# Output projection of two mixers: partial sums of three token tiles kept in PSUM banks, and two places for the first MLP weights' work

## The chip, the cores and the metric

One core of a Trainium2 chip. The metric is the device time of one execution in microseconds (us); lower is better. Engines: PE (TensorE, matmul), DVE (VectorE), ACT (ScalarE), POOL (GpSimd), SP (SyncE, which issues most DMAs). Time before: 1218.78 us, median of 3 runs (1217.87 to 1219.89).

## The reference

A two-layer decoder trunk for 512 tokens of width 1024, in float32.

```python
for layer in range(DEPTH):                      # DEPTH = 2
    hn = rmsnorm(h, mix_norm[layer])
    if layer % 2 == 0:
        h = h + moba_nsa_mixer(hn, ...)         # 8 MoBA and 8 NSA heads
    else:
        h = h + fox_mixer(hn, ...)              # 16 heads, forgetting attention
    h = h + sqrelu_mlp(rmsnorm(h, mlp_norm[layer]), mlp_w1[layer], mlp_w2[layer])
return rmsnorm(h, final_norm)
```

Both mixers end in `o @ w_out`: all heads' outputs, 512 x 1024, times a 1024 x 1024 matrix. `sqrelu_mlp` is `relu(h @ w1)**2 @ w2` with 4096 hidden columns.

## The kernel before

The stages follow each other: mixer 0 to about 315 us, its MLP to about 640, the forgetting attention ("fox") to about 885, the second MLP to the end. The residual stream stands in four tiles `x0` to `x3` of 128 tokens x 1024. A float32 product is made of three matmuls (`mm3`, L142 to L144): each operand is split into a rounded high part and a low part, and high x low, low x high and high x high are added in one PSUM bank. High parts of weights are copies on ACT (L100), low parts a subtraction on DVE or POOL (L107); `whl` holds both.

PSUM has eight banks here: four tags (`acc`, `s`, `pt`, `o`) of two buffers each. `acc` takes sums of projections, `s` logits (L544, L583), `pt` transposes (L566, L395) and also logits of fox, `o` the heads' outputs (L639, L662).

Output projection (`out_proj`): heads go in pairs, of which there are eight; a pair is 128 rows of `w_out`. For given pairs, token tile t and half n of the 1024 columns, three matmuls per pair add into one `acc` bank, and DVE adds the bank to `x` (L711, 128x512). An operation `o45:012` does this for pairs 4 and 5 and tiles 0 to 2. Mixer 0 ends with pairs 2 and 3, whose heads come last; fox ends with 6 and 7. A pair's output is split before: in mixer 0 by ACT (L680), DVE (L681) and POOL (L533, L689), in fox by ACT (L672) and DVE (L673).

Then comes the MLP: each tile x is squared and summed on ACT (L383), a scale `nr` comes of it (L386 to L388, DVE), x is multiplied by it and the norm's weights (L390, DVE, `xn`), transposed on PE through `pt` banks (L395), and copied to float16 high and low parts by ACT (L398) and DVE (L399).

The first MLP weights are prepared within the mixer before: `s0` to `s3` (mixer 0 only) load one of four 128-column blocks and square it on ACT (L441) for a scale; `x` loads them again, and `z0` to `z3` (`prepare_part`, `up_split`) make their high float16 part on ACT (L477) and the low part on DVE (L478). An instruction tied by `issue_after` stands in its engine's queue no earlier than the one named. `prepare_part` ties its two to `a_last` and `ev_last`; `ev_last` is the last addition to x so far.

The order of all this is written in two strings, whose words run from left to right: the scheduler sets each instruction by the order written, the ties and the readiness of its data, and each engine then works off its queue in order. Other words: `n`, `m` attention of a pair of NSA or MoBA heads, `k`, `q`, `v` projections, `c` compressed branch, `t` scales, `p` a pair of fox heads.

Of the kernel before, what the change touches and what calls it, by code (L numbers as in the profile page):

```python
# [12 lines left out]
ALU = mybir.AluOpType  # L13
# [31 lines left out]

MIX0_ORDER = "c0 k1 q1 s0 n0 v1 s1 v0 s2 k0 s3 n1 m1 c1 t m0 k2 n2 o45:0123 o0:0123 n3 k3 m2 m3 o17:0123 o6:012 o23:0 x0 z0 o23:1 z1 o6:3 z2 o23:2 z3 o23:3"

FOX_ORDER = "v0 f k0 k1 p0 k2 v1 p1 k3 p2 o01:0123 k4 v2 p3 k5 p4 k6 v3 p5 k7 p6 o23:0123 p7 o45:012 o67:0 x1 z0 o67:1 z1 o45:3 z2 o67:2 z3 o67:3"

# [5 lines left out]
class Trunk:  # L55
    def __init__(self, ctx, tc, I, out):
# [3 lines left out]
        self.phase = "D"  # L60
        self.wout = {}
        e = ctx.enter_context
        PS = bass.MemoryType.PSUM
# [23 lines left out]
    def split(self, srcs, shape, pool):  # L87
# [10 lines left out]
        def parts(squares=None):  # L98
            hl = (pool or self.whl).tile([P, 2, W_RAW], FR, tag="whl", name=self.nm("whl"))
            nc.scalar.activation(hl[:, 0, :n], raw[:, :n], AF.Copy)  # L100
            if squares is not None:
                c, scratch, out = squares
                scratch = (hl[:, 1] if scratch is None else scratch)[:, :n].rearrange("p (a b) -> p a b", a=a)
                nc.scalar.activation(scratch[:, :, :c], rv[:, :, :c], AF.Square, accum_out=out)
            eng = nc.gpsimd if self.phase[self.pieces % len(self.phase)] == "P" else nc.vector
            self.pieces += 1
            eng.tensor_tensor(hl[:, 1, :n], raw[:, :n], hl[:, 0, :n].bitcast(F32), op=ALU.subtract)  # L107
            hv = hl[:, :, :n].rearrange("p t (a b) -> p t a b", a=a)
            return [(hv[:, 0, i], hv[:, 1, i]) for i in range(a)]
# [378 lines left out]
    def prepare_mlp(self, layer):  # L488
# [5 lines left out]
        def part(f):  # L494
            self.first_up.extend(self.up_split(raws[f:f + 1], self.up_first[layer][:, :, f:f + 1], tiles[f:f + 1], [(self.a_last, self.ev_last)]))
        self.prepare_part = part
# [38 lines left out]
    def softmax(self, passes, band, gate):  # L535
# [4 lines left out]
        for qi in range(NT):  # L540
            w = P * (qi + 1)
            ps = self.psum("s")
            for i, (q, k) in enumerate(passes):
                nc.tensor.matmul(ps[:, :w], q[:, qi * P:(qi + 1) * P], k[:, :w],  # L544
                                 start=i == 0, stop=i == len(passes) - 1)
            seg = pt[:, SEG[qi]:SEG[qi] + w]
# [7 lines left out]
    def transpose_p(self, p):  # L554
# [4 lines left out]
        for off, js in BANKS:  # L559
            pt = self.psum("pt")  # L560
            w = 0
            for j, c in js:
                for qi in range(j, NT):
                    a = SEG[qi] + j * P
                    b = c + (qi - j) * P
                    nc.tensor.transpose(pt[:, b:b + P], p[:, a:a + P], self.ident)  # L566
                    w = max(w, b + P)
# [4 lines left out]
    def softmax_t(self, passes, band):  # L572
# [6 lines left out]
        for qi in (3, 2, 1, 0):  # L579
            w = P * (qi + 1)  # L580
            ps = self.psum("s" if qi % 2 else "pt")
            for i, (q, k) in enumerate(passes):
                nc.tensor.matmul(ps[:, :w], q[:, qi * P:(qi + 1) * P], k[:, :w],  # L583
                                 start=i == 0, stop=i == len(passes) - 1)
            seg = pt[:, SEG[qi]:SEG[qi] + w]
# [105 lines left out]

    def out_proj(self, w, arg, os, hs, late, pools={}):

        nc = self.nc
        pairs, tiles = ([int(a) for a in part] for part in arg.split(":"))
        phase = self.phase
        if tiles[0] == 0:
            for i in pairs:
                self.phase = "P" if i in late else "D"
                self.wout[i] = self.rows(w, P * i, 1, pools.get(i))[0]  # L700
                self.phase = phase
        for t in tiles:
            for n in range(2):
                ps = self.psum("acc")
                for k, i in enumerate(pairs):
                    o, wc = os[i], self.wout[i]
                    self.mm3(ps, (o[:, 0, t * P:(t + 1) * P], o[:, 1, t * P:(t + 1) * P]),
                             (wc[0][:, n * 512:(n + 1) * 512], wc[1][:, n * 512:(n + 1) * 512]),
                             k == 0, k == len(pairs) - 1)
                hv = hs[t][:, n * 512:(n + 1) * 512]  # L710
                self.ev_last = nc.vector.tensor_tensor(hv, ps, hv, op=ALU.add)  # L711

# [63 lines left out]
    def mixer0(self):  # L776
# [5 lines left out]
        with ExitStack() as cx:  # L782
# [210 lines left out]
            def step(op, arg):  # L993
# [21 lines left out]
                elif op == "m":  # L1015
                    o[int(arg)] = moba_pair(int(arg), *k[int(arg)])
                elif op == "o":
                    self.out_proj(wo, arg, o, hs, ())

# [148 lines left out]
    def mlp(self, layer, hs, final=None):  # L1168
# [6 lines left out]
        with ExitStack() as cx:  # L1175
# [161 lines left out]
            def down(s, act):  # L1337
                bs = combos(act)
                if s < 6:
                    late = 4 * [(self.up_done[3],)] if ahead < 3 else [(done,) for done in self.up_done]  # L1340
                    if s == 1 and ahead < 4:
                        self.up_squares(*loaded[3], up_sq[1], self.parts_last)
                        scale[3] = up_scale(3, "acc")
                    up_split(s + 2, self.added if s else self.first_low, late if s + 2 < 4 else None)
                bank = {}
# [77 lines left out]
    def fox(self, hs):  # L1423
# [5 lines left out]
        with ExitStack() as cx:  # L1429
# [124 lines left out]
            def step(op, arg):  # L1554
# [11 lines left out]
                elif op == "p":  # L1566
                    pair(int(arg), st[int(arg)])
                elif op == "o":
                    if int(arg.split(":")[0][-1]) not in o:
                        with self.tc.issue_after(self.mm_last.ins):  # L1570
                            behind()
                    self.out_proj(wo, arg, o, hs, (6, 7), {7: last})

# [43 lines left out]
```

## Time and profile before

| | |
|---|---|
| median of 3 runs | 1218.78 us |
| the profiled execution | 1221.25 us |
| its span | 1219.5 us |
| granted PE clock | 0.994 |
| additions to x (L711) | 72, median 689 ns |

A row of a timeline gives start (us from the span's start), duration in us, engine, line, operation, output and inputs with shapes, and in square brackets the idle time of the engine just before it with what ended it. In a table of windows each engine has its busy time and number of instructions; PEclk is the granted clock as a share of the full one.

### The profile page before, as it was taken

The numbers are of one execution on the slowest core, as the hardware profiler recorded it, in microseconds if no ns is written. First come the engines' busy times: TensorE is split into PE (matmuls) and PEld (weight loads), VectorE is DVE, ScalarE is ACT, GpSimd is POOL, SyncE is SP. The second block draws the span as 40 slices with busy tenths as digits, with TensorE's granted clock in tenths as the row PEclk, the third lists the DMA queues.
The fourth block names the chain that finished last, engine by engine and source line by source line (L and its number), as shares of the span: only waits on it lengthen the run. The fifth ranks groups of instructions, "written<-read, shape, count | busy, mean of one in ns | idle before, by whom it ended". The sixth has DMA issues, their size and how long they took to land.

```text
span 1219.5 us, 17282 instructions
## 1 busy us (share of the span) xinstructions
PE 1183.5 (97%) x6197; PEld 870.3 (71%) x6197; DVE 937.9 (77%) x1741; ACT 734.3 (60%) x1347; POOL 323.5 (27%) x387
## 2 busy tenths in 40 slices
PE   9999998998999999999999999999999999999997
PEld 7878987886755665665588888787675666656666
DVE  6867778897879778876977685777787697779865
ACT  6456756784386676767524874676357555656442
POOL 3434555461041111121001643434003102201104
PEclk9999999999999999999999999999999999999999
DMA  8972242124323474456105473636644233442101
GB/s 234 330 227 80 70 129 70 44 61 121 87 87 115 127 207 140 117 158 212 33 1 154 105 161 88 153 92 139 183 138 138 87 104 87 138 121 71 68 1 70
DMA packets 204531, 144.78 MB, mean 119 GB/s; under 512 B 48484, under 2 KB 179724, under 8 KB 204445
## 3 DMA queue, kind: packets, MB, share of 16 engines
q1 hardware_dynamic: 204284, 143.44, 41.7%
q8 instruction: 49, 0.80, 0.3%
q14 instruction: 38, 0.30, 0.1%
q10 hardware_dynamic: 160, 0.23, 0.1%
HBM read 130.76 MB, written 7.64 MB: 113 GB/s over the span
## 4 chain that ended last, share of the span: by engine, by line
PE 77%; DVE 11%; DMA 5%; ACT 4%; issue 2%; POOL 1%; ACTq 0%; DVEq 0%; POOLq 0%; SPq 0%
PE acc L142 14%; PE acc L143 14%; PE acc L144 14%; PE s L1361 12%; PE o L1361 6%; PE pt L1361 3%; PE o L639 2%; PE pt L566 2%; PE s L544 2%; DVE whl L107 1%; DMA w<-in_mlp_w 1%; DMA HT<-HL 1%; PE s L144 1%; PE s L143 1%; PE s L142 1%
## 5 line engine op out<-in xcount | busy, mean ns | idle before, releaser
L142 PE MATMUL acc<-x,w 128*128 128x512 f16 (+1 forms) x512 | 187.8, 368 | 0.4 <-ACT r L1250 0.3
L143 PE MATMUL acc<-x,w 128*128 128x512 f16 (+1 forms) x512 | 187.7, 367 | 0.3 <-DVE nr L387 0.3
L144 PE MATMUL acc<-x,w 128*128 128x512 f16 (+1 forms) x512 | 187.5, 367 | 0.0
L1361 PE MATMUL s<-whl,sp 128*128 128x512 f32 x672 | 177.9, 406 | 0.0
L1361 PEld LDWEIGHTS s<-whl,sp 128*128 128x128 f32 x672 | 126.3, 188 | 31.0 <-DVE x L1370 0.5
L1309 ACT ACTIVATE whl<-w 128x1024 fp32r<-128x1024 f32 x98 | 100.3, 1048 | 65.5 <-DVE w L1315 40.5
L1370 DVE SCALAR_TENSOR_TENSOR x<-s,nr,x 128x512 f32<-128x512 f32 x112 | 82.6, 745 | 67.7 <-PE s L1361 67.5
L1310 DVE TENSOR_TENSOR whl<-w,whl 128x1024 fp32r<-128x1024 f32 x98 | 121.5, 1257 | 9.8 <-ACT whl L1309 9.7
L100 ACT ACTIVATE whl<-raw 128x1024 fp32r<-128x1024 f32 (+1 forms) x75 | 77.6, 1043 | 45.6 <-PE acc L144 16.6
L142 PEld LDWEIGHTS <-w 128*128 128x128 f16 x576 | 57.3, 100 | 57.6 <-issue 10.3
L1276 POOL TENSOR_TENSOR t<-act 128x512 f32<-128x512 f32 x14 | 24.8, 1772 | 274.0 <-ACT act L1252 251.0
L142 PE MATMUL acc<-xhi,whl 128*128 128x512 f32 x240 | 94.8, 395 | 1.7 <-DVE QS L529 0.8
L144 PEld LDWEIGHTS <-w 128*128 128x128 f16 x576 | 56.5, 98 | 55.6 <-issue 4.5
L144 PE MATMUL acc<-xhi,whl 128*128 128x512 f32 x240 | 94.2, 393 | 0.5 <-DVE whl L107 0.4
L143 PE MATMUL acc<-xlo,whl 128*128 128x512 f32 x240 | 94.0, 391 | 0.0
L143 PEld LDWEIGHTS <-w 128*128 128x128 f16 x576 | 56.6, 98 | 51.6 <-issue 4.5
L1361 PE MATMUL o<-whl,sp 128*128 128x512 f32 x336 | 84.8, 396 | 2.0 <-DVE x L1370 1.4
L107 DVE TENSOR_TENSOR whl<-raw,whl 128x1024 fp32r<-128x1024 f32 (+2 forms) x58 | 72.7, 1259 | 14.0 <-ACT whl L100 10.1
L1315 DVE TENSOR_TENSOR w<-w,w 128x1024 f32<-128x1024 f32 x56 | 72.2, 1289 | 5.0 <-DMA w<-in_mlp_w 4.6
L1250 ACT ACTIVATE r<-acc,upsc 128x512 f32<-128x512 f32 x44 | 30.0, 681 | 76.1 <-PE acc L144 76.0
L1361 PEld LDWEIGHTS o<-whl,sp 128*128 128x128 f32 x336 | 62.9, 188 | 16.5 <-DVE x L1370 1.8
L549 ACT ACTIVATE P<-P,sst 128x384 f32<-128x384 f32 (+2 forms) x96 | 53.4, 557 | 22.4 <-DVE sst L548 21.8
(346 smaller groups left out, 2910.0 us busy)
## 6 DMA issues: line engine op xcount, KB each, us to landing
w<-in_mlp_w SPq DMA_DIRECT2D x140, 512.0 KB
raw<-in_odd_w_in SPq DMA_DIRECT2D x22, 512.0 KB
raw<-in_even_w_in SPq DMA_DIRECT2D x20, 512.0 KB
band<-bias_dram SPq DMA_DIRECT2D x24, 256.0 KB
bias_dram<-bias_rows SPq DMA_DIRECT2D x16, 320.0 KB
raw<-in_even_w_out SPq DMA_DIRECT2D x8, 512.0 KB
raw<-in_mlp_w SPq DMA_DIRECT2D x8, 512.0 KB
raw<-in_odd_w_out SPq DMA_DIRECT2D x8, 512.0 KB
```

What stands on the lines that cost most here:

```text
L100: nc.scalar.activation(hl[:, 0, :n], raw[:, :n], AF.Copy)
L107: eng.tensor_tensor(hl[:, 1, :n], raw[:, :n], hl[:, 0, :n].bitcast(F32), op=ALU.subtract)
L142: mm(ps, ahl[0], bhl[0], start=first, stop=False)
L143: mm(ps, ahl[0], bhl[1], start=False, stop=False)
L144: self.mm_last = mm(ps, ahl[1], bhl[0], start=False, stop=last)
L549: nc.scalar.activation(seg, seg, AF.Exp, bias=mn, scale=-1.0, accum_out=sm)
L1250: nc.scalar.activation(r, ps, AF.Relu, scale=undo[:, 1, f:f + 1])
L1309: nc.scalar.activation(t[:, 0], src, AF.Copy)
L1310: nc.vector.tensor_tensor(t[:, 1], src, t[:, 0].bitcast(F32), op=ALU.subtract)
L1315: nc.vector.tensor_tensor(out, a_, b_, op=op)
L1361: mm = lambda l, r, first, last: nc.tensor.matmul(ps, l, r, start=first, stop=last, skip_group_check=True)
L1370: self.added = nc.vector.scalar_tensor_tensor(hv, ps, by_token(t), hv, op0=ALU.mult, op1=ALU.add)
```

## The change

In both strings the operation `o` is taken apart at the ends:

- `w45` loads and splits the output weights of pairs 4 and 5 (`out_rows`); before, the first `o` of a pair did this.
- `a6:1:s` opens the sums of pair 6 and tile 1 in the two banks of tag `s` and leaves them open; the matmuls are tied behind the last matmul, logit or transpose that uses the tag.
- `b23:1` adds pairs 2 and 3 to tile 1's open banks, and then DVE adds them to x.
- `o623:3` is as before, with all pairs left over for tile 3 in one sum.

At each end three tiles hold `acc`, `s` and `pt`, six banks. Additions to x fall from 16 to 8 at each end. The number of matmuls is the same.

Besides: `s0` to `s3` stand later in mixer 0. For the second layer `prepare_part` ties to the last high copy on ACT (`high_last`) in place of `a_last`. In the first MLP one tie of a weight split is dropped. `h` names the place where fox's follow-up (`behind`) is issued.

```diff
-MIX0_ORDER = "c0 k1 q1 s0 n0 v1 s1 v0 s2 k0 s3 n1 m1 c1 t m0 k2 n2 o45:0123 o0:0123 n3 k3 m2 m3 o17:0123 o6:012 o23:0 x0 z0 o23:1 z1 o6:3 z2 o23:2 z3 o23:3"
-FOX_ORDER = "v0 f k0 k1 p0 k2 v1 p1 k3 p2 o01:0123 k4 v2 p3 k5 p4 k6 v3 p5 k7 p6 o23:0123 p7 o45:012 o67:0 x1 z0 o67:1 z1 o45:3 z2 o67:2 z3 o67:3"
+MIX0_ORDER = "c0 k1 q1 n0 v1 v0 s0 k0 s1 n1 s2 m1 s3 c1 t m0 k2 n2 w45 o45:0123 w0 o0:0123 n3 k3 m2 m3 w17 o17:0123 w6 a6:0:acc a6:1:s a6:2:pt w23 x0 z0 z1 b23:0 z2 b23:1 z3 b23:2 o623:3"
+FOX_ORDER = "v0 f k0 k1 p0 k2 v1 p1 k3 p2 w01 o01:0123 k4 v2 p3 k5 p4 k6 v3 p5 k7 p6 w23 o23:0123 p7 w45 a45:0:acc a45:1:s a45:2:pt w67 x1 z0 z1 h b67:0 z2 b67:1 z3 b67:2 o4567:3"
...
-            nc.scalar.activation(hl[:, 0, :n], raw[:, :n], AF.Copy)
+            self.high_last = nc.scalar.activation(hl[:, 0, :n], raw[:, :n], AF.Copy)
...
-            self.first_up.extend(self.up_split(raws[f:f + 1], self.up_first[layer][:, :, f:f + 1], tiles[f:f + 1], [(self.a_last, self.ev_last)]))
+            self.first_up.extend(self.up_split(raws[f:f + 1], self.up_first[layer][:, :, f:f + 1], tiles[f:f + 1], [((self.high_last if layer else self.a_last), self.ev_last)]))
...
+    def out_part(self, ps, n, t, pairs, os, first, last):
+        for k, i in enumerate(pairs):
+            o, wc = os[i], self.wout[i]
+            self.mm3(ps, (o[:, 0, t * P:(t + 1) * P], o[:, 1, t * P:(t + 1) * P]),
+                     (wc[0][:, n * 512:(n + 1) * 512], wc[1][:, n * 512:(n + 1) * 512]),
+                     first and k == 0, last and k == len(pairs) - 1)
+
+    def out_proj(self, op, arg, os, hs):
...
+            if op == "a":
+                behind = {"acc": self.mm_last, "s": self.logit_last, "pt": self.turn_last or self.logit_last}[tag[0]]
+                for n in range(2):
+                    self.part[t, n] = ps = self.psum(tag[0])
+                    with self.tc.issue_after(behind.ins):
+                        self.out_part(ps, n, t, pairs, os, True, False)
+            elif op == "b":
+                for i in pairs:
+                    for n in range(2):
+                        with self.tc.issue_after(self.mm_last.ins):
+                            self.out_part(self.part[t, n], n, t, [i], os, False, i == pairs[-1])
+                for n in range(2):
+                    self.out_add(self.part.pop((t, n)), n, t, hs)
...
+    def out_add(self, ps, n, t, hs):
+        hv = hs[t][:, n * 512:(n + 1) * 512]
+        self.ev_last = self.nc.vector.tensor_tensor(hv, ps, hv, op=ALU.add)
...
-                    up_split(s + 2, self.added if s else self.first_low, late if s + 2 < 4 else None)
+                    up_split(s + 2, self.added if s else self.first_low, late if s + 2 < 4 and not (s and ahead < 4) else None)
```

The lines of the changed kernel are one higher up to the output projection (L107 becomes L108, L478 becomes L479), and the addition to x is L734 in place of L711.

**DVE, end of mixer 0.** `PTl` is the low part of the last head pair's transposed attention weights, which PE needs for that pair's output (`o_532`); `whl_555` and `whl_557` are the output weights of pairs 2 and 3; `o_506` is the last pair's output on its way to being split. Before:

```order
L711 TENSOR_TENSOR x3_127<-acc_544_3424,x3_127 128x512
L711 TENSOR_TENSOR x3_127<-acc_545_3432,x3_127 128x512
L107 TENSOR_TENSOR whl_555_3477<-raw_554_3475,whl_555_3477 128x1024
L107 TENSOR_TENSOR whl_557_3482<-raw_556_3480,whl_557_3482 128x1024
L569 TENSOR_TENSOR PTl_528_3332<-pt_531_3347,PTh_527_3331 128x256
L711 TENSOR_TENSOR x0_108<-acc_548_3445,x0_108 128x512
L681 TENSOR_TENSOR o_506_3234<-o_519_3288,o_506_3234 64x512
L711 TENSOR_TENSOR x0_108<-acc_549_3450,x0_108 128x512
L681 TENSOR_TENSOR o_506_3234<-o_532_3352,o_506_3234 64x512
```

Now:

```order
L734 TENSOR_TENSOR x3_127<-acc_544_3424,x3_127 128x512
L570 TENSOR_TENSOR PTl_528_3332<-pt_531_3347,PTh_527_3331 128x256
L734 TENSOR_TENSOR x3_127<-acc_545_3432,x3_127 128x512
L108 TENSOR_TENSOR whl_555_3471<-raw_554_3469,whl_555_3471 128x1024
L108 TENSOR_TENSOR whl_557_3476<-raw_556_3474,whl_557_3476 128x1024
L682 TENSOR_TENSOR o_506_3234<-o_519_3288,o_506_3234 64x512
L682 TENSOR_TENSOR o_506_3234<-o_532_3352,o_506_3234 64x512
L479 SCALAR_TENSOR_TENSOR w16_558_3479<-w1_559_3480,up_st_83,w16_558_3479 128x1024
L479 SCALAR_TENSOR_TENSOR w16_558_3479<-w1_560_3482,up_st_83,w16_558_3479 128x1024
L734 TENSOR_TENSOR x0_108<-acc_548_3445,x0_108 128x512
```

`PTl` has moved ahead of the two weight splits, the additions for pair 6 are gone, and two low parts of the first MLP weights stand ahead of the first addition.

**DVE, end of the forgetting attention.** `whl_1282` before and `whl_1274` now are the output weights of pair 5; `w16` are the first MLP weights; `O` is a split output. Before:

```order
L711 TENSOR_TENSOR x3_127<-acc_1260_8507,x3_127 128x512
L673 SCALAR_TENSOR_TENSOR O_1270_8579<-o_1269_8554,vscale_6288,O_1270_8579 128x512
L107 TENSOR_TENSOR whl_1282_8628<-raw_1281_8626,whl_1282_8628 128x1024
L711 TENSOR_TENSOR x0_108<-acc_1283_8631,x0_108 128x512
L711 TENSOR_TENSOR x0_108<-acc_1284_8639,x0_108 128x512
```

Now:

```order
L734 TENSOR_TENSOR x3_127<-acc_1252_8491,x3_127 128x512
L479 SCALAR_TENSOR_TENSOR w16_1285_8667<-w1_1286_8668,up_st_83,w16_1285_8667 128x1024
L674 SCALAR_TENSOR_TENSOR O_1262_8563<-o_1261_8538,vscale_6272,O_1262_8563 128x512
L479 SCALAR_TENSOR_TENSOR w16_1285_8667<-w1_1287_8670,up_st_83,w16_1285_8667 128x1024
L108 TENSOR_TENSOR whl_1274_8612<-raw_1273_8610,whl_1274_8612 128x1024
L674 SCALAR_TENSOR_TENSOR O_1291_8705<-o_1290_8680,vscale_6272,O_1291_8705 128x512
L734 TENSOR_TENSOR x0_108<-acc_1275_8615,x0_108 128x512
```

Two low parts of the MLP weights have come between the addition to x3 and the weight split of pair 5.

**ACT, in mixer 0.** `w1` rows are the squares, `P` rows exponentials of the softmax, `whl` high parts of weights, `ptch` a copy of transposed compressed weights. Before:

```order
L753 ACTIVATE QS_125_1100<-acc_123_1071 64x512
L549 ACTIVATE P_135_1149,sst_136_1150<-P_135_1149,sst_136_1150 128x384
L441 ACTIVATE w1_212_1719,up_st_83<-w1_212_1719 128x1024
L100 ACTIVATE whl_193_1522<-raw_191_1518 128x1024
L1163 ACTIVATE ptch_107_982<-pt_106_977 128x512
L549 ACTIVATE P_135_1149,sst_136_1150<-P_135_1149,sst_136_1150 128x512
```

Now:

```order
L550 ACTIVATE P_134_1146,sst_135_1147<-P_134_1146,sst_135_1147 128x256
L442 ACTIVATE w1_210_1713,up_st_83<-w1_210_1713 128x1024
L101 ACTIVATE whl_191_1516<-raw_189_1512 128x1024
L550 ACTIVATE P_134_1146,sst_135_1147<-P_134_1146,sst_135_1147 128x384
L550 ACTIVATE P_134_1146,sst_135_1147<-P_134_1146,sst_135_1147 128x512
L442 ACTIVATE w1_261_1970,up_st_83<-w1_261_1970 128x1024
L1188 ACTIVATE ptch_107_982<-pt_106_977 128x512
L550 ACTIVATE P_145_1205,sst_146_1206<-P_145_1205,sst_146_1206 128x128
```

Where one square stood among the exponentials of the first NSA pair there are now two (the second and third of four); the first stands ahead of them, among the copies of the compressed branch, and the fourth eight rows further on.

More of the change, by code (lines that the diff above doesn't have):

```diff
@@ L61, in __init__ @@
         self.wout = {}
+        self.part = {}
         e = ctx.enter_context
@@ L543, in softmax @@
             for i, (q, k) in enumerate(passes):
-                nc.tensor.matmul(ps[:, :w], q[:, qi * P:(qi + 1) * P], k[:, :w],
-                                 start=i == 0, stop=i == len(passes) - 1)
+                self.logit_last = nc.tensor.matmul(ps[:, :w], q[:, qi * P:(qi + 1) * P], k[:, :w],
+                                                   start=i == 0, stop=i == len(passes) - 1)
             seg = pt[:, SEG[qi]:SEG[qi] + w]
@@ L565, in transpose_p @@
                     b = c + (qi - j) * P
-                    nc.tensor.transpose(pt[:, b:b + P], p[:, a:a + P], self.ident)
+                    self.turn_last = nc.tensor.transpose(pt[:, b:b + P], p[:, a:a + P], self.ident)
                     w = max(w, b + P)
@@ L582, in softmax_t @@
             for i, (q, k) in enumerate(passes):
-                nc.tensor.matmul(ps[:, :w], q[:, qi * P:(qi + 1) * P], k[:, :w],
-                                 start=i == 0, stop=i == len(passes) - 1)
+                self.logit_last = nc.tensor.matmul(ps[:, :w], q[:, qi * P:(qi + 1) * P], k[:, :w],
+                                                   start=i == 0, stop=i == len(passes) - 1)
             seg = pt[:, SEG[qi]:SEG[qi] + w]
@@ L690, in split_o, with out_rows @@
         return hl
-    def out_proj(self, w, arg, os, hs, late, pools={}):
-        nc = self.nc
-        pairs, tiles = ([int(a) for a in part] for part in arg.split(":"))
+    def out_rows(self, w, pairs, late=(), pools={}):
         phase = self.phase
[L697 to L711, printed above, removed]
+        for i in pairs:
+            self.phase = "P" if i in late else "D"
+            self.wout[i] = self.rows(w, P * i, 1, pools.get(i))[0]
+            self.phase = phase
@@ new lines, in out_part @@
+    def out_part(self, ps, n, t, pairs, os, first, last):
[5 more added lines that the diff above has]
+    def out_proj(self, op, arg, os, hs):
+        pairs, tiles, *tag = arg.split(":")
+        pairs = [int(a) for a in pairs]
+        for t in (int(a) for a in tiles):
+            if op == "a":
[5 more added lines that the diff above has]
+            elif op == "b":
+                for i in pairs:
+                    for n in range(2):
[3 more added lines that the diff above has]
+                    self.out_add(self.part.pop((t, n)), n, t, hs)
+            else:
+                for n in range(2):
+                    ps = self.psum("acc")
+                    self.out_part(ps, n, t, pairs, os, True, True)
+                    self.out_add(ps, n, t, hs)
@@ L1016, in step @@
                     o[int(arg)] = moba_pair(int(arg), *k[int(arg)])
-                elif op == "o":
-                    self.out_proj(wo, arg, o, hs, ())
+                elif op == "w":
+                    self.out_rows(wo, [int(i) for i in arg])
+                elif op in "oab":
+                    self.out_proj(op, arg, o, hs)
             for s in MIX0_ORDER.split():
@@ L1435, in fox @@
             a1 = cx.enter_context(self.tc.tile_pool(name="attf1", bufs=1))
+            self.turn_last = None
             self.p_up = a1.tile([P, NT], F32, name="pup")
@@ L1567, in step @@
                     pair(int(arg), st[int(arg)])
[L1568 to L1572, printed above, removed]
+                elif op == "w":
+                    self.out_rows(wo, [int(i) for i in arg], (6, 7), {7: last})
+                elif op == "h":
+                    with self.tc.issue_after(self.mm_last.ins):
+                        behind()
+                elif op in "oab":
+                    self.out_proj(op, arg, o, hs)
             for s in FOX_ORDER.split():
```

## The prediction

> **What bounds the kernel now.** I read the page first (busy shares, chain), then a table by windows of the two places that the change rewrites, then the timelines of TensorE (PE), VectorE (DVE), ScalarE (ACT) and GpSimd (POOL) there.
>
> ```profile
> PE 1183.5 (97%) x6197; PEld 870.3 (71%) x6197; DVE 937.9 (77%) x1741; ACT 734.3 (60%) x1347; POOL 323.5 (27%) x387
> PE 77%; DVE 11%; DMA 5%; ACT 4%; issue 2%; POOL 1%; ACTq 0%; DVEq 0%; POOLq 0%; SPq 0%
> ```
>
> PE is busy 97% of the span, and three quarters of the chain that ends last run through it. The change has the same matmuls, so it can win only where PE stands still. The windows show where that is: the end of mixer 0 (286 to 318 us) and the end of the forgetting attention (856 to 888 us).
>
> ```profile
> core 0: us, PE busy (x) PEld busy (x) DVE busy (x) ACT busy (x) POOL busy (x), PEclk, DMA share, GB/s
> 286.00:298.00 12.00, 9.66 (x41) 6.73 (x40) 9.63 (x14) 7.73 (x9) 3.83 (x4) 1.00 0.60 158
> 298.00:310.00 12.00, 11.08 (x50) 8.32 (x50) 11.04 (x20) 2.98 (x6) 0.00 (x0) 1.00 0.54 149
> 310.00:314.00 4.00, 1.77 (x9) 1.00 (x8) 3.94 (x10) 2.80 (x7) 0.00 (x0) 1.00 0.74 203
> 314.00:318.00 4.00, 3.99 (x22) 3.16 (x23) 4.00 (x14) 1.16 (x3) 0.00 (x0) 0.57 0.56 151
> 856.00:870.00 14.00, 13.01 (x69) 8.99 (x68) 6.79 (x10) 4.15 (x5) 2.77 (x1) 1.00 0.59 140
> 870.00:882.00 12.00, 11.56 (x52) 8.79 (x53) 11.60 (x22) 5.15 (x9) 0.00 (x0) 1.00 0.79 246
> 882.00:888.00 6.00, 5.31 (x37) 3.83 (x36) 5.99 (x13) 3.21 (x8) 0.00 (x0) 1.00 0.59 167
> ```
>
> From 298 on DVE is as full as PE (11.04 of 12, 3.94 of 4), and at 310 to 314 PE works 1.77 of 4 us while DVE works 3.94: DVE is the bound of the tail. What it holds up, in PE's own timeline:
>
> ```profile
> 290.81 0.38 PE L639 MATMUL o<-PTl,vm 128*128 128x256 f32 x1 [1.23 <-DVE PTl L569]
> 291.41 0.50 PE L142 MATMUL acc<-whl,O 128*128 128x512 f32 x1 [0.22 <-DVE x L711]
> 292.60 0.50 PE L142 MATMUL acc<-whl,O 128*128 128x512 f32 x1 [0.23 <-DVE x L711]
> 294.05 0.50 PE L142 MATMUL acc<-whl,O 128*128 128x512 f32 x1 [0.48 <-DVE x L711]
> 295.89 0.47 PE L142 MATMUL acc<-whl,O 128*128 128x512 f32 x1 [0.17 <-DVE x L711]
> 298.07 0.39 PE L142 MATMUL acc<-whl,O 128*128 128x512 f32 x1
> 298.30 0.39 PE L143 MATMUL acc<-whl,O 128*128 128x512 f32 x1
> 304.37 0.50 PE L142 MATMUL acc<-whl,O 128*128 128x512 f32 x1 [0.88 <-DVE x L711]
> 312.67 0.65 PE L395 MATMUL pt<-ident,xn 128*128 128x128 f32 x4 [1.55 <-DVE nr L386]
> 314.01 1.09 PE L395 MATMUL pt<-ident,xn 128*128 128x128 f32 x4 [0.69 <-DVE nr L387]
> ```
>
> Matmuls of 0.39 us start every 0.23 us (298.07, 298.30), so a matmul that starts only when the one before it has ended has already lost 0.16, and the bracket comes on top. The eight brackets add up to 5.45; with 8 x 0.16 the loss is **6.7 us**. Besides, the clock is 0.57 at 314 to 318, which costs at most 4.00 x 0.43 = 1.7 us.
>
> **The change part by part.**
>
> *End of mixer 0.* The sums of three token tiles stay open in six banks, with the early pair added first and the late pairs later, so the evictions (additions to x) of that pair fall away: eight of 0.69 us here, eight at the other end. The five waits on x at 291 to 304 end with them, as every group after the kept ones finds its bank long opened. The 1.23 wait goes for another reason: DVE's low copy of the transposed weights of the attention (PTl) now stands ahead of the two L107, which filled 2.96 us:
>
> ```profile
> 287.45 2.96 DVE L107 TENSOR_TENSOR whl<-raw,whl 128x1024 fp32r<-128x1024 f32 x2
> 293.30 1.29 DVE L711 TENSOR_TENSOR x<-acc,x 128x512 f32<-128x512 f32 x2
> 302.38 1.28 DVE L478 SCALAR_TENSOR_TENSOR w<-w,up_st,w 128x1024 f16<-128x1024 f32 x1
> 310.00 1.41 DVE L390 SCALAR_TENSOR_TENSOR xn<-x,nr,g 128x512 f32<-128x512 f32 x2
> 311.93 0.68 DVE L399 TENSOR_TENSOR x<-pt,x 128x512 f16<-128x512 f32 x1
> 291.27 0.67 DVE L681 TENSOR_TENSOR o<-o,o 64x512 f32<-64x512 f32 x1
> 291.23 0.59 ACT L680 ACTIVATE o<-o 64x512 f32<-64x512 f32 x1 [2.19 <-PE o L639]
> 293.36 0.62 POOL L533 TENSOR_SCALAR O<-o 128x512 fp32r<-128x512 f32 x1 [5.16 <-DVE o L681]
> 294.06 1.30 POOL L689 TENSOR_TENSOR O<-o,O 128x512 fp32r<-128x512 f32 x1
> ```
>
> Two things are late next. (1) The low half of the last head pair, which takes ACT 0.59, DVE 0.67, POOL 0.62 and 1.30 after that pair's last product, now with both L107 ahead of the DVE step. By the new order DVE starts the L107 when ACT's high copies are done (about 289.5), leaves them at 292.4, splits two heads to 293.7, and POOL ends at 295.7. PE has 14 matmuls (3.3 us) between that last product (291.1) and the first product that needs it, with some overhead at 294.9: a wait of 0.8. Bounds: 0 (POOL ends at 295.36 now and PE doesn't wait) and 2.96, both L107. (2) The transposes of the norm. From the first addition to x on, DVE has 8 additions (0.60 apart, 4.8), two L478 (2.4), four L390 (2.7), small ones (0.7) and the L399 that frees the first pt bank (0.6): 11.2, to 11.9 with waits for ACT's squares of x. PE has 45 matmuls and 8 transposes in that time, 10.5 + 0.5 = 11.0. So the second tile's transposes start 0.2 to 0.9 late, ACT's copy (0.60) stands before the first MLP product, and the other half follows the same way, about 0.5 more: I take 2.0. Bounds: 0 (both engines level), and 1.55 + 0.69 + 2 x 0.16 = 2.6, what this place costs now. The clock I leave as it is, since 2.0 idle follow where 2.24 idle preceded the 0.57. Sum: 6.7 - 0.8 - 2.0 = **3.9 us gained**.
>
> In the windows the clock fell after a stretch in which PE was never idle for more than 1.55 us at once. The Trainium skill, page "TensorE: Matmul & The Clock Gate", section "Part 1: The HAM clock gate", has the clock halved after at least one idle window of about 3.4 us. Read strictly, that gives full clock after the change, as no single gap would be that long, and 1.7 us more gain; the row at 314 speaks against so strict a reading, so I don't count it.
>
> *End of the forgetting attention.*
>
> ```profile
> 857.53 0.51 PE L143 MATMUL acc<-whl,O 128*128 128x512 f32 x1 [0.36 <-DVE whl L107]
> 859.05 0.50 PE L142 MATMUL acc<-whl,O 128*128 128x512 f32 x1 [0.32 <-DVE x L711]
> 870.25 0.50 PE L142 MATMUL acc<-whl,O 128*128 128x512 f32 x1 [0.56 <-DVE x L711]
> 881.66 0.50 PE L142 MATMUL acc<-whl,O 128*128 128x512 f32 x1 [0.20 <-DVE x L711]
> 883.60 1.29 PE L395 MATMUL pt<-ident,xn 128*128 128x128 f32 x8 [0.28 <-DVE xn L390]
> 856.26 1.22 DVE L107 TENSOR_TENSOR whl<-raw,whl 128x1024 fp32r<-128x1024 f32 x1
> 855.60 0.74 DVE L673 SCALAR_TENSOR_TENSOR O<-o,vscale,O 128x512 fp32r<-128x512 f32 x1
> ```
>
> Less is to be had: the waits on x (0.32, 0.56, 0.20) with 3 x 0.16 are 1.6 us. Against it stand two new waits. The new tie puts two L478 on DVE ahead of the L107 for which PE waits at 857.53: from the end of the x3 sums DVE now has one addition (0.7), L478, split of O (0.7), L478, L107, that is 0.7 + 1.2 + 0.7 + 1.2 + 1.2 = 5.0 us, against 12 matmuls (2.8 us) of PE: a wait of about 2.2 instead of 0.5, so +1.7. Bounds: nothing, if the L478's place is filled by other PE work, and two L478, 2.6. Second, one half of K of the last pair now comes after four masks on DVE; I put 0.4 on it (bounds 0 and 0.69, one addition). At the transposes two L478 less stand in DVE's tail, six adds more come late; I take no change there (bounds -0.5 and +2.0, as at the other end). Sum: -1.6 + 1.7 + 0.4 = **0.5 lost**.
>
> *Squares of the first MLP weights.*
>
> ```profile
> 77.18 1.06 ACT L441 ACTIVATE w<-w 128x1024 f32<-128x1024 f32 x1 [2.43 <-DMA w<-in_mlp_w]
> 79.73 0.50 PE L142 MATMUL acc<-xhi,whl 128*128 128x512 f32 x1 [0.79 <-DVE QS L529]
> 102.33 1.06 ACT L441 ACTIVATE w<-w 128x1024 f32<-128x1024 f32 x1 [1.36 <-DMA w<-in_mlp_w]
> ACT w L441 <- DMA w<-in_mlp_w: 13.0, 6, 3.8
> ```
>
> The square at 77.18 waited for its load and delayed PE at 79.73 by 0.79 + 0.16; that goes, about 1.0. In return three of the four squares (1.06, with the read 1.2) now stand among the softmax rows at 97 to 115 us, where the third one's load can be issued only when the second's square has freed its buffer. I take 1.0 for it, one wait of the size of the one at 102.33 less what ACT idles there anyway; bounds 0 and 3 x (3.8 + 1.2) = 15. Net **0**. The dropped tie in the first MLP and POOL's few moved rows change no row that PE waits for: 0.
>
> *Sum.* -3.9 + 0.5 + 0 = -3.4. The profiled execution took 1221.25 (span 1219.5), 2.47 above the median 1218.78; I take the difference as it is: 1217.85 for such an execution, **1215.4** at the median.
>
> **Rivals.** What a measurement of this kernel can tell from no change is about 0.2%, 2.4 us.
>
> *B, the held banks move the wait.* With six banks held the norm's transposes cannot start before the last pt sum is evicted, and each nr waits for an add and for ACT's square behind it (1.06 + 0.19). If one square is exposed at each end, 2 x 1.25 comes on top: -0.9, **1217.9**. For it speaks DVE at 3.94 of 4.00 in 310 to 314; against it that tile 3's 18 matmuls (4.2 us) cover there. This is also what the Trainium skill's page "Perfetto Trace Analysis", section "Matmuls", warns of: independent groups should go round the banks so that one's evacuation overlaps the next one's matmuls. Here the round of two banks is what waited at 291 to 304, so rule and row differ for the groups, and agree for the transposes.
>
> *C, slower.* The moved squares: ACT takes its queue in order, and behind a square that waits for its load stand the exponentials on which PE's transposes and products hang. If each of three squares costs PE a load wait of 1.36 and itself (1.25), 7.8 come on top: +4.4, **1223.2**. It decides from 5.8 us, that is 1.9 for each square. For it: such squares wait 13.0 us in all in the run before, 3.8 at the longest; against it: ACT is idle 40% of the span.
>
> *D, all waits at both ends go*, with clock: -6.7 - 1.7 - 2.1 and no new ones, -10.5; with half the new ones about -9, **1209.8**. DVE's full tail speaks against it.
>
> **How the numbers follow.** Forecast 0.42 (1212 to 1216.3), B 0.31 (1216.3 to 1221.2), C 0.14, D 0.13. Faster by over 0.2%: 0.42 + 0.13 = 0.55; within: 0.31; slower: 0.14. The range takes in forecast and B, the nearer half of D, and C only at its edge: 1209 to 1221.5.
>
> **What would show it.** In the changed profile: no wait on x of more than 0.2 at the end of mixer 0, no wait on PTl; a wait on O's low half of 0.8; a gap before the second tile's transposes of about 1 us; 0.57 again after it or not; at the second end a PE wait on L108 (now L107) of about 2 us, which is the boldest claim; between 78 and 120 us a sum of PE waits as before. If L108 is not waited for, or if the gap before the first MLP product is over 3 us, the sum is wrong.

## The result, and the profile after

| | before | changed |
|---|---|---|
| median of 4 runs | 1218.33 us | 1227.24 us |
| all runs | 1217.87 to 1219.89 | 1225.48 to 1228.8 |
| profiled execution (span) | 1221.25 (1219.5) | 1225.99 (1224.3) |

The ratio is 1.0070, 95% interval 1.0051 to 1.0090: the change makes the kernel 6 to 11 us slower. The forecast was 1215.4, with a range up to 1221.5.

Engine totals of the page after:

```profile
PE 1183.9 (97%) x6197; PEld 873.2 (71%) x6197; DVE 931.9 (76%) x1725; ACT 735.0 (60%) x1347; POOL 322.3 (26%) x387
```

PE has the same 6197 instructions and the same busy time to 0.4 us, and DVE the 16 additions less. So the 4.8 us between the two spans are idle time and a lower clock. To find the places I set each row of PE in one trace beside the same row in the other and watched how the difference of their starts (after minus before) runs along the span: -0.7 us at 13 us, -1.3 at 74, +2.1 at 196, +1.3 from 220 to 270, +0.4 after mixer 0's end (333), +0.4 still at 820, +4.8 after the forgetting attention's end (902) and from there to the last row. The squares' stretch loses 3.4 (from -1.3 to +2.1), mixer 0's end gains 0.9 instead of 3.9, and the second end loses 4.4 instead of 0.5. Two steps are none of these. The -1.3 ahead of 74 us lies ahead of the squares, and run 1 below, which has the squares back, has it too. The 0.8 between 196 and 220 is a matter of the two executions: from 204.8 us on the kernel before ran at half clock (a granted clock of 0.50) for 3.4 us, and the changed one did not.

Table of windows, after (busy time and instructions of each engine, PEclk the granted clock):

```profile
core 0: us, PE busy (x) PEld busy (x) DVE busy (x) ACT busy (x) POOL busy (x), PEclk, DMA share, GB/s
...
100.00:120.00 20.00, 17.02 (x113) 15.38 (x112) 10.96 (x44) 14.52 (x40) 9.28 (x13) 0.91 0.43 119
280.00:299.00 19.00, 16.02 (x80) 12.64 (x78) 14.31 (x18) 10.73 (x14) 5.61 (x4) 0.96 0.25 77
299.00:305.00 6.00, 5.82 (x15) 4.62 (x16) 2.89 (x5) 1.15 (x2) 0.12 (x1) 0.56 1.16 296
...
860.00:865.00 5.00, 1.79 (x8) 1.12 (x6) 5.00 (x4) 0.55 (x1) 2.37 (x1) 0.91 0.37 78
865.00:871.00 6.00, 5.73 (x14) 3.97 (x16) 0.21 (x1) 1.15 (x1) 0.00 (x0) 0.50 0.52 145
```

At both ends the same pair of windows stands: one in which PE waits while DVE and POOL work (860 to 865: PE 1.79 of 5, DVE 5.00), and behind it one in which PE is busy but at half clock (0.56, 0.50).

**Mixer 0's end.** PE, POOL and DVE, after:

```profile
296.98 0.50 PE L143 MATMUL acc<-whl,O 128*128 128x512 f32 x1 [1.76 <-POOL O L534]
...
299.18 0.79 PE L145 MATMUL acc<-whl,O 128*128 128x512 f32 x1 [1.40 <-POOL O L690]
299.77 0.63 PE L143 MATMUL acc<-whl,O 128*128 128x512 f32 x1
300.20 0.63 PE L144 MATMUL acc<-whl,O 128*128 128x512 f32 x1
```

```profile
289.60 0.62 POOL L534 TENSOR_SCALAR O<-o 128x512 fp32r<-128x512 f32 x1 [13.01 <-PE acc L145]
290.30 1.30 POOL L690 TENSOR_TENSOR O<-o,O 128x512 fp32r<-128x512 f32 x1
295.23 1.70 POOL L534 TENSOR_SCALAR O<-o 128x512 fp32r<-128x512 f32 x1 [3.63 <-DVE o L682]
297.01 2.11 POOL L690 TENSOR_TENSOR O<-o,O 128x512 fp32r<-128x512 f32 x1
```

```profile
293.74 1.40 DVE L682 TENSOR_TENSOR o<-o,o 64x512 f32<-64x512 f32 x2
295.17 2.83 DVE L479 SCALAR_TENSOR_TENSOR w<-w,up_st,w 128x1024 f16<-128x1024 f32 x2
```

No product waits for x any more, nor for PTl. But the split of the last pair's output, which took POOL 0.62 and 1.30 us at 289.60, takes the same rows 1.70 and 2.11 at 295.23, just while DVE makes two low parts of the MLP weights (L479). PE waits 1.76 for the high half and 1.40 for the low half, and then starts a product every 0.43 us (299.77, 300.20) instead of every 0.23.

**The forgetting attention's end.** PE, DVE and POOL, after:

```profile
861.16 0.63 PE L143 MATMUL pt<-whl,O 128*128 128x512 f32 x2
865.27 0.79 PE L144 MATMUL acc<-whl,O 128*128 128x512 f32 x1 [3.48 <-DVE whl L108]
865.86 0.63 PE L145 MATMUL acc<-whl,O 128*128 128x512 f32 x1
```

```profile
859.27 1.28 DVE L479 SCALAR_TENSOR_TENSOR w<-w,up_st,w 128x1024 f16<-128x1024 f32 x1
860.47 0.75 DVE L674 SCALAR_TENSOR_TENSOR O<-o,vscale,O 128x512 fp32r<-128x512 f32 x1
861.13 2.95 DVE L479 SCALAR_TENSOR_TENSOR w<-w,up_st,w 128x1024 f16<-128x1024 f32 x1
864.00 1.21 DVE L108 TENSOR_TENSOR whl<-raw,whl 128x1024 fp32r<-128x1024 f32 x1
```

```profile
860.62 2.37 POOL L108 TENSOR_TENSOR whl<-raw,whl 128x1024 fp32r<-128x1024 f32 x1 [6.15 <-DVE w L479]
```

The wait on L108 is there as forecast, but 3.48 us long: the second L479 needs 2.95 us where the first needed 1.28. POOL's L108 stands beside it until 862.99.

**The squares.** ACT and PE, after:

```profile
101.05 0.71 ACT L550 ACTIVATE P<-P,sst 128x512 f32<-128x512 f32 x1
...
103.70 1.06 ACT L442 ACTIVATE w<-w 128x1024 f32<-128x1024 f32 x1 [1.84 <-DMA w<-in_mlp_w]
...
104.87 0.60 ACT L1188 ACTIVATE ptch<-pt 128x512 fp32r<-128x512 f32 x1
```

```profile
102.30 0.44 PE L545 MATMUL s<-KS,QS 128*128 128x384 f32 x1 [0.71 <-DVE sst L549]
...
103.71 0.33 PE L567 MATMUL pt<-ident,P 128*128 128x128 f32 x1 [0.79 <-POOL P L552]
105.52 0.72 PE L988 MATMUL o<-ptch,vc 128*128 128x512 f32 x2 [1.48 <-ACT ptch L1188]
```

The same wait and the same stretch before:

```profile
105.10 0.73 PE L965 MATMUL o<-ptch,vc 128*128 128x512 f32 x2 [0.27 <-ACT ptch L1163]
```

```profile
100.00:120.00 20.00, 19.63 (x140) 17.34 (x138) 14.13 (x51) 14.64 (x40) 9.85 (x14) 1.00 0.32 89
```

ACT stands 1.84 us at a square whose load is late; behind it stands the copy (L1188) that PE needs at 105.52, and PE waits 1.48 us for it instead of 0.27. PE works 17.02 of the 20 us from 100 to 120, at 0.91 of the clock, instead of 19.63 at 1.00.

### The profile page after: what moved, and what is told of

Read it like the earlier page. It is cut to its first block, busy times and chain, and to the rows that moved or that the text cites. A ratio compares the mean times of both kernels' runs of the same rounds, so it can differ in the third digit from the quotient of the medians.

```text
span 1224.3 us, 17256 instructions
## 1 busy us (share of the span) xinstructions
PE 1183.9 (97%) x6197; PEld 873.2 (71%) x6197; DVE 931.9 (76%) x1725; ACT 735.0 (60%) x1347; POOL 322.3 (26%) x387
## 5 line engine op out<-in xcount | busy, mean ns | idle before, releaser
L1335 DVE TENSOR_TENSOR whl<-w,whl 128x1024 fp32r<-128x1024 f32 x98 | 121.5, 1257 | 10.2 <-ACT whl L1334 10.1
L108 DVE TENSOR_TENSOR whl<-raw,whl 128x1024 fp32r<-128x1024 f32 (+2 forms) x58 | 72.4, 1255 | 15.1 <-ACT whl L101 11.3
L550 ACT ACTIVATE P<-P,sst 128x128 f32<-128x128 f32 (+1 forms) x96 | 53.2, 556 | 23.8 <-DVE sst L549 23.4
```

Of the source, the lines that this page charges most:

```text
L550: nc.scalar.activation(seg, seg, AF.Exp, bias=mn, scale=-1.0, accum_out=sm)
L1335: nc.vector.tensor_tensor(t[:, 1], src, t[:, 0].bitcast(F32), op=ALU.subtract)
```

## The experiments

Times of one kernel spread over 5 to 10 us, more than most single effects, so each run below gives its ratio to the kernel before, measured on the same chip, and beside it what the same rows of PE show at the place in question. The rows are of one execution each, so a stretch of lower clock that comes in one execution and not in another is in them too. Diffs are against the changed kernel unless said otherwise, and three dots stand for what is left out.

**1. The squares back.**

```diff
-MIX0_ORDER = "c0 k1 q1 n0 v1 v0 s0 k0 s1 n1 s2 m1 s3 c1 t ..."
+MIX0_ORDER = "c0 k1 q1 s0 n0 v1 s1 v0 s2 k0 s3 n1 m1 c1 t ..."
```

> The changed kernel with only its squares back where they stood before (in the order of mixer 0: one ahead of the first NSA pair, the others between it and the next key steps). Theory 1: the squares behind late transfers, two of them ahead of the copy of the transposed compressed weights, cost PE the 1.48 us wait on that copy, smaller waits beside it and about 1 us of lower clock, together the 2.1 to 2.7 us by which PE's rows fall back between 86 and 196 us; undone, the time falls by 2 to 3 us against the changed kernel, to about 1225, and the half clock between 107 and 109 us goes. Theory 2 (the forecast's): the squares cost as much in either place; no change, within 1 us of 1227.

1.0034 (1.0022 to 1.0046): 0.36% below the change's 1.0070, some 4 us. PE's rows at 181 us come 3.7 us earlier than in the changed kernel, and 2.6 from 220 us on: this execution ran at half clock for 3.4 us from 204.0 on, the changed kernel's did not. Theory 1, and by the time more than its 2 to 3.

**2. The second end back.**

```diff
-FOX_ORDER = "... w45 a45:0:acc a45:1:s a45:2:pt w67 x1 z0 z1 h b67:0 z2 b67:1 z3 b67:2 o4567:3"
+FOX_ORDER = "... w45 o45:012 h w67 o67:0 x1 z0 o67:1 z1 o45:3 z2 o67:2 z3 o67:3"
...
-... [((self.high_last if layer else self.a_last), self.ev_last)] ...
+... [(self.a_last, self.ev_last)] ...
```

> The changed kernel with only the end of the forgetting attention back in its old form (products of pairs 4 and 5 for three tiles first, no held banks, old ties of the first MLP weights). Theory 1: this end as changed loses the 4.4 us by which PE's rows fall back around 865 us, so undone the time falls by 4 to 5 us against the changed kernel, to about 1223. Theory 2 (the forecast's): this end is worth +0.5 only, and the loss lies elsewhere; undone it is within 1 us of 1227.

1.0035 (1.0020 to 1.0050), again some 4 us; PE's rows gain 5.2 us at this end. Theory 1.

**3. Mixer 0's end back.**

```diff
-... w6 a6:0:acc a6:1:s a6:2:pt w23 x0 z0 z1 b23:0 z2 b23:1 z3 b23:2 o623:3"
+... w6 o6:012 w23 o23:0 x0 z0 o23:1 z1 o6:3 z2 o23:2 z3 o23:3"
```

> The changed kernel with only the end of mixer 0 back in its old form (pair 6 for three tiles first, its additions to x, then pairs 2 and 3). Theory 1 (PE's offsets): this end as changed gains only 0.9 us, since the waits on the split of O and the half clock from 299 to 304 us eat what the eight waits on x gave; undone the time rises by about 1 us against the changed kernel, to 1228. Theory 2 (the forecast's size): the gain is 3.9 us; undone the time rises to about 1231. Theory 3: the held banks cost more than they bring: it falls.

1.0075 (1.0051 to 1.0098): not to be told from the changed kernel's time, and the two intervals together are too wide to exclude 3.9 us. PE's rows stand 5.76 us apart ahead of this end and 5.66 behind it, so the new end gains 0.1 us (0.9 against the trace of before). Theory 1; in the rows a gain of 3.9 is not there.

**4. Only the tie back.** Held banks and order strings stay.

```diff
-... [((self.high_last if layer else self.a_last), self.ev_last)] ...
+... [(self.a_last, self.ev_last)] ...
```

> The changed kernel with one tie undone: the first MLP weights of the second layer are again tied to the last product by ScalarE instead of the last high part of weights, which puts the weight split of pair 5 (L108) ahead of both low parts of the MLP weights (L479) on DVE and leaves the held banks as they are. Theory 1: the 3.65 us wait on L108 at 865 us and the 5 us at half clock behind it come from that order; undone, the wait falls under 1 us, the half clock goes, and the time falls by 4.5 to 6 us against the changed kernel, to 1221 to 1223. Theory 2: the wait moves to the last pair's split of O (L674), now behind both low parts: the time falls by 2 us or less. Theory 3: the split waits for its transfer or for the banks, not for DVE's order: no change.

1.0010 (0.9998 to 1.0022): 0.6% below the change, 7 us, more than undoing the whole end brings. DVE and PE:

```profile
861.90 1.22 DVE L108 TENSOR_TENSOR whl<-raw,whl 128x1024 fp32r<-128x1024 f32 x1
863.03 2.48 DVE L479 SCALAR_TENSOR_TENSOR w<-w,up_st,w 128x1024 f16<-128x1024 f32 x2
```

```profile
863.13 0.63 PE L143 MATMUL pt<-whl,O 128*128 128x512 f32 x2
863.60 0.40 PE L144 MATMUL acc<-whl,O 128*128 128x512 f32 x1
```

L108 is done before PE asks for it, the wait of 3.48 is gone whole, the clock stays up, and the two low parts take 2.48 together. POOL's L108 stands beside the second of them now (from 864.67) and takes 3.06 us instead of 2.37, but PE does not wait for it. PE's rows gain 6.8 us at this end, 1.6 more than with the old end of run 2: that is what the held banks themselves bring here, as much as the prediction gave for the waits on x. Against the kernel before, run 4's rows gain 2.3 us; 0.8 of that run 2 has too, at 838 to 846 us, before these sums begin.

**5. Tie and squares back** (the edits of 1 and 4 together).

> The changed kernel with both undone: the tie of the second layer's first MLP weights, and the squares' places. If the two costs lie apart and add, as theory 1 has it (7 us and 4 to 5 us in the runs with one undone each), the time is near 1216, 0.2 to 0.4% below the kernel before. If the squares' gain was only a shift of the slack that the second end also used, the time stays at the 1220 to 1221 of the run with the tie alone.

0.9977 (0.9967 to 0.9987), median 1216.20: 3 us faster than the kernel before. The two costs add: 0.36% and 0.60% of 0.70% leave -0.26%, and -0.23% is measured.

**6. Low parts later at mixer 0's end** (on top of 5).

```diff
-... w23 x0 z0 z1 b23:0 z2 b23:1 ...
+... w23 x0 b23:0 z0 z1 z2 b23:1 ...
```

> As the run with tie and squares undone, and at mixer 0's end the first two low parts of the MLP weights (L479 on DVE) come behind the two additions to x0 instead of ahead of them, so that POOL splits the last pair's output (L534, L690) with DVE idle. Theory 1 (the two engines stretch each other): POOL's rows go back from 1.70 and 2.11 us to about 0.6 and 1.3, PE's waits on them from 1.76 and 1.40 us to about 0.9 and 0.8, the lower clock behind them goes, and the time falls by 3 to 4 us. Theory 2: POOL's rows are long because of their own operands; they keep their length, no gain. Theory 3: the low parts are then late for the MLP: waits on w16 at its start, and the time rises.

0.9965 (0.9952 to 0.9978). POOL and PE:

```profile
292.24 0.62 POOL L534 TENSOR_SCALAR O<-o 128x512 fp32r<-128x512 f32 x1 [3.64 <-DVE o L682]
292.94 1.27 POOL L690 TENSOR_TENSOR O<-o,O 128x512 fp32r<-128x512 f32 x1
```

```profile
292.91 0.50 PE L143 MATMUL acc<-whl,O 128*128 128x512 f32 x1 [0.68 <-POOL O L534]
...
294.26 0.50 PE L145 MATMUL acc<-whl,O 128*128 128x512 f32 x1 [0.62 <-POOL O L690]
```

```profile
308.31 1.31 PE L396 MATMUL pt<-ident,xn 128*128 128x128 f32 x8 [2.00 <-DVE nr L388]
```

Theory 1 in every row: 0.62 and 1.27 on POOL, and no half clock behind the shorter waits. PE's rows gain 4.6 us up to the end of the output projection. Then 1.6 is lost again, as theory 3 expected a loss, but not where it expected it: PE waits not for the weights but for the norm. DVE now has the low parts behind the additions, and the second tile's transposes wait 2.00 us for it instead of 0.98. 3.0 us are left at this place. The runs can't tell it from run 5 (the intervals overlap).

**7. Pair 2 first** (on top of 5): a new operation adds one pair into a held bank without closing it.

```diff
+            elif op == "d":
+                for n in range(2):
+                    with self.tc.issue_after(self.mm_last.ins):
+                        self.out_part(self.part[t, n], n, t, pairs, os, False, False)
...
-... z0 z1 b23:0 z2 b23:1 z3 b23:2 ...
+... z0 z1 d2:0 d2:1 d2:2 b3:0 z2 b3:1 z3 b3:2 ...
```

> As the run with tie and squares undone, and at mixer 0's end PE multiplies pair 2 for all three held tiles (18 products, 4.1 us) before it starts on pair 3, whose output POOL is still splitting. Nothing else moves: DVE's low parts and POOL's split still run together. Theory 1: the two waits of 1.76 and 1.40 us lie under the 12 products moved ahead (2.8 us), 0.8 us of wait or less is left, the clock stays up, and the time falls by 4 to 5 us against that run. Theory 2 (the wait only moves): the additions to x0 come 2.8 us later, and the waits of the first transposes on the norm (0.98 and 0.69 us) grow by as much: no change.

0.9963 (0.9947 to 0.9980). POOL's rows stay at 1.70 and 2.13; PE:

```profile
295.52 0.50 PE L145 MATMUL acc<-whl,O 128*128 128x512 f32 x1 [0.69 <-POOL O L690]
...
305.25 1.23 PE L396 MATMUL pt<-ident,xn 128*128 128x128 f32 x8 [1.53 <-ACT xn L384]
307.88 1.77 PE L396 MATMUL pt<-ident,xn 128*128 128x128 f32 x8 [1.40 <-DVE x L400]
```

The wait on the split shrinks to 0.69, as theory 1 has it, and a part of theory 2 comes true as well: the transposes wait 1.53 and 1.40 instead of 0.98 and 0.69, and behind them, from 308.1 us on, PE runs at half clock for 3.4 us. PE's rows gain 2.4 us here, not 4 to 5.

**8. Both of them** (on top of 5, with the operation of 7).

```diff
-... z0 z1 b23:0 z2 b23:1 z3 b23:2 ...
+... d2:0 d2:1 d2:2 b3:0 z0 z1 z2 b3:1 z3 b3:2 ...
```

> The two edits of the runs before together: pair 2 first, and the first low parts of the MLP weights behind the additions to x0. Theory 1: no wait on POOL's split is left after either, so the second brings nothing more than the first, within 1 us of the run with pair 2 first. Theory 3: the low parts, now later by the products moved ahead too, are late for the MLP's first products: 1 us or more above that run.

0.9983 (0.9969 to 0.9997): above 6 and 7 in its value, and the trace says why: PE's first transposes wait 3.47 us for ACT (xn L384) and the next 2.02 for DVE's nr, with half clock for 10.2 us from 307.0 on, and PE's rows lose 1.2 us at this place. It is the loss of theory 3, but again the waits are for the norm and not for the weights.

**9. The squares tied instead of moved** (on top of 4).

```diff
-self.up_ahead(0, 0, int(arg), None)
+self.up_ahead(0, 0, int(arg), self.copy_last if arg in "12" else None)
...
-nc.scalar.activation(th, pt, AF.Copy)
+self.copy_last = nc.scalar.activation(th, pt, AF.Copy)
```

> The changed kernel with the tie of the second layer undone, and the second and third square tied behind ScalarE's copy of the transposed compressed weights (L1188); their loads keep their place in the list. Theory 1 (the squares' cost is that ScalarE stands at two late transfers ahead of that copy): the copy comes early, PE's 1.48 us wait on it and the lower clock behind it go, and the time falls by most of the 4 us that the old places gave, from 1220.8 (tie alone) to 1217 to 1218. Theory 2 (the cost is in the order of the loads, or elsewhere in mixer 0): it stays within 1 us of 1220.8, and other waits take the place of that one.

0.9982 (0.9967 to 0.9997), median 1217.31: 0.28%, 3.4 us, below the tie alone. ACT and PE:

```profile
101.30 0.60 ACT L1188 ACTIVATE ptch<-pt 128x512 fp32r<-128x512 f32 x1
101.80 1.05 ACT L442 ACTIVATE w<-w 128x1024 f32<-128x1024 f32 x1
```

```profile
101.96 0.73 PE L988 MATMUL o<-ptch,vc 128*128 128x512 f32 x2
```

The copy runs at 101.30 instead of 104.87, PE does not wait for it, and PE is busy all 20 us from 100 to 120 at full clock:

```profile
100.00:120.00 20.00, 20.00 (x152) 18.90 (x151) 14.54 (x55) 18.33 (x50) 10.84 (x16) 1.00 0.47 132
```

Theory 1: it is the place in ACT's queue, since the loads kept theirs but for a row or two.

**10. The wait filled.** Nothing undone; 15 products with a stationary tile of zeros, which add nothing to the sum.

```diff
...
         mm(ps, ahl[0], bhl[0], start=first, stop=False)
+        for _ in range(15 if fill is not None else 0):
+            mm(ps, fill, bhl[0], start=False, stop=False)
...
+                     self.zeros if i == 5 and t == 2 and n and self.turn_last is None else None)
...
```

> The changed kernel with nothing undone, and in the forgetting attention's end 15 products with a stationary tile of zeros put on PE (they add nothing to a held bank) just ahead of the products that wait 3.65 us for the weight split of pair 5, so that PE works for about 3.4 us of that wait. If the 5 us at half clock behind that wait come from PE's standing still, the rows behind it run at full clock and PE's rows after this end come 2 to 2.5 us earlier against the changed kernel (1.0050 of the time before instead of 1.0070), though the wait on DVE is as long as before. If the clock falls for another reason (the load on DVE, POOL or the transfers there), it falls as before, and the time stays at 1.0070 or rises.

PE of that kernel (lines two higher), and its window behind the wait:

```profile
864.08 3.66 PE L145 MATMUL pt<-whl,zeros 128*128 128x512 f32 x15
867.75 0.50 PE L146 MATMUL acc<-whl,O 128*128 128x512 f32 x1
868.09 0.39 PE L147 MATMUL acc<-whl,O 128*128 128x512 f32 x1
868.32 0.39 PE L146 MATMUL acc<-whl,O 128*128 128x512 f32 x1
```

```profile
866.00:872.00 6.00, 5.99 (x36) 4.05 (x36) 1.70 (x2) 1.15 (x1) 0.00 (x0) 1.00 0.43 126
```

DVE's second low part is as long as before (2.98), L108 as late, and PE gets no further in that time. Yet the products behind start every 0.23 us at clock 1.00, and PE's rows come 2.5 us earlier against the changed kernel. The half clock stands behind this wait in all three traces that have it unfilled (the changed kernel, runs 1 and 3), and not here. So it comes from PE's standing still, and costs 2.5 us here beside the wait itself, as far as one execution shows it. In the time, 1.0063 (1.0042 to 1.0084), it drowns: neither the 1.0050 that was expected nor 1.0070 is excluded.

**11. A middle way at mixer 0's end** (on top of 5, with the operation of 7).

```diff
-... z0 z1 b23:0 z2 b23:1 z3 b23:2 ...
+... z0 d2:0 d2:1 b3:0 z1 z2 b3:1 z3 b23:2 ...
```

> As the run with tie and squares undone, and at mixer 0's end a middle way: pair 2 first for two of the held tiles (6 products, 1.4 us, moved ahead of pair 3), one low part of the MLP weights ahead of the additions to x0 and the other behind. If waits on POOL's split and waits on the norm trade one for one, it ends where the runs with all of pair 2 first and with the low parts later ended (0.9963 to 0.9965). If the trade has a best point between, both waits come under 0.7 us each and it ends 1 to 2 us lower, at 0.995 or less.

0.9962 (0.9946 to 0.9978), median 1214.68, PE's rows gain 2.3 us. The waits on the split are 0.37 and 0.63, but one transpose waits 1.40 for DVE, and half clock for 3.4 us follows from 310.1 on. This point between is no better: what is taken off POOL's split returns at the norm, where DVE has little room (busy 5.51 of 6 us from 303 to 309 in run 7).

Runs 5 to 9 and 11 beat both kernels, with intervals below 1, runs 8 and 9 by the least; 6, 7 and 11, 4 to 5 us below the kernel before, can't be told apart.

## Why the prediction was wrong

It had the right places and the right instructions, and mis-sized three terms, all in the same direction.

*Mixer 0's end, +3.9 forecast.* The 6.7 us of eight waits did go. (1) "A wait of 0.8" on the last pair's output, bounds 0 and 2.96, became two waits of 1.76 and 1.40 in the brackets, 3.6 by the starts of the rows (294.83 to 296.98 and 297.32 to 299.18, each less the usual 0.23). The sum had POOL's 0.62 and 1.30 from rows during which DVE added from PSUM; beside L479, which reads two tiles of SBUF, they took 1.70 and 2.11. Run 6 shows that this is the cause. (2) The transposes: 2.0 forecast, 0.98 + 0.69 and twice 0.16, another 0.3 behind, 2.3 measured. (3) "The clock I leave as it is": the 0.57 behind the transposes went (1.00 from 305 on, +1.7), and half clock came behind the new waits, 12 products of 0.43 instead of 0.23, -2.4. Together 6.7 - 3.6 - 2.3 + 1.7 - 2.4 = 0.1, against 0.1 (run 3) and 0.9 (before) measured.

*The second end, -0.5 forecast.* The gain of 1.6 is right (runs 2 and 4). The wait, "about 2.2 instead of 0.5", was 3.6 with its 0.16, outside its bound, because one L479 was taken as 1.2 and took 2.95 beside POOL's L108; K's half cost 0.33 (forecast 0.4); and the half clock behind the wait, 2.4, was not in the sum at all. At the transposes no change was forecast; there and at the first MLP products PE waits 0.98 + 0.13 us instead of 0.28 + 0.33, another 0.5. 1.6 - 3.1 - 0.3 - 2.4 - 0.5 = -4.7; measured -4.4. Run 4 shows that the tie is the whole cause of the wait, run 10 that the clock is a cost of its own.

*The squares, 0 forecast.* The wait of 0.79 at the old place went. The price in return, "one wait of the size of the one at 102.33 less what ACT idles there", 1.0 in bounds of 0 to 15, was 3.4 us net by the rows, 3.4 to 4.4 by the runs. What I left out is that the queue decides: the idle time of ACT, 40% of the span, was counted as room for the squares, but 1.84 us of it were spent waiting at one of them, and the copy behind it could not go ahead (run 9 moves it ahead, and the cost is gone). Rival C had this mechanism and 0.14; it asked 5.8 us of it to end slower, as it took the other two terms for right.

Rival B (held banks move the wait to the norm) is small, 0.3 us at mixer 0's end and at most 0.5 at the second, where it asked 1.25 at each. That the banks work shows in run 5: without the tie and with the squares back, the same held banks give 0.9977. That this is near the forecast's 0.9972 is chance: against the kernel before, run 5's rows gain 0.6 us at mixer 0's end, where the forecast had 3.9, and 2.6 at the second, where it had a loss of 0.5.

On the two engines, the Trainium skill has a rule that the prediction should have weighed: page "SBUF — State Buffer", section "Who interferes with whom", says that a DVE instruction with two SBUF inputs and a GpSimd instruction that reads SBUF exclude each other, and that the later one waits until the earlier is done. The trace agrees: POOL's L108 ends at 862.99, and 1.28 more is 864.27, where the stretched L479 ends at 864.08; the first L479 at 295.17 would end at 296.45, and 0.62 more is 297.07, where the stretched L534 ends at 296.93. By that rule, as an estimate from these rows, this end alone would have been forecast 1.7 us (2.95 - 1.28) worse.

## What to carry to other kernels

When a tie or an order list moves an instruction, read what its engine's neighbour does in that moment, not only what stands in its own queue: two rows that each fit may not fit together. A wait of PE of some 3.5 us cost its length and, in the changed kernel, about 2.4 us of lower clock behind it (in run 3's trace the same wait was followed by half clock for 3.4 us and not 6.8, seven slow products and not twelve, some 1.4 us), so a new wait is to be priced as two terms, the second with a range. And an engine that idles 40% of the time can still hold the bound up for 1.5 us where a row that waits for a transfer stands ahead of one that PE needs.

## What was not expected of the hardware

The half clock doesn't need one long wait. At mixer 0's end 1.92 + 1.63 us (by the starts of the rows) and 0.6 us of work between are followed by it in all seven traces with that order (the changed kernel and runs 1, 2, 4, 5, 9, 10), for 3.4 us in runs 1 and 4 and for 6.8 us in the others. And where the waits are shorter it depends on the execution: at the second NSA pair PE waits 0.51, 0.90 and 0.60 us (brackets, alike to 0.03) in the same rows in the changed kernel and in runs 1 and 4, and the windows behind those waits read, in this order (after, run 1, run 4; columns as above):

```profile
208.00:212.00 4.00, 3.49 (x22) 2.65 (x23) 3.69 (x18) 3.87 (x14) 4.00 (x8) 1.00 0.65 209
```

```profile
205.00:209.00 4.00, 3.97 (x20) 3.15 (x19) 3.21 (x14) 3.51 (x10) 4.00 (x9) 0.70 0.57 189
```

```profile
210.00:214.00 4.00, 4.00 (x17) 3.46 (x16) 3.22 (x13) 3.31 (x10) 4.00 (x8) 0.50 0.64 210
```

Clocks of 1.00, 0.70 and 0.50 behind the same waits: no half clock, half clock for 3.4 us and for 6.8 us. Between the changed kernel and run 4, whose orders differ only 600 us later, PE's rows move 3.2 us from 162 to 242 us, 1.6 of it here and 1.6 in the same way behind two waits of 1.06 and 0.94 us at 188 to 190 us, after which run 4's clock reads 0.67 (192 to 196 us) and the changed kernel's 1.00. In all these traces the stretches of half clock ahead of the last 20 us are 3.4, 6.8 or, once, 10.2 us long. That the clock differs by execution fits the page "TensorE: Matmul & The Clock Gate" of the Trainium skill, section "Part 1: The HAM clock gate", in that its activity window runs free of the kernel; that waits of 1.92 and 1.63 us suffice doesn't fit its one idle window of about 3.4 us read as one gap. Much of the spread between executions of one kernel may come from here: in run 7 the executions with a granted clock of 0.997, 0.996 and 0.991 took 1210.96, 1212.19 and 1217.24 us. That was not tested further.
